# Block transposes of a triangular inverse moved from TensorE to VectorE, and residual parts and a first down product of a mixture of experts moved in the order

## The chip, the core and the metric

The kernel runs on one core of one Trainium2 chip. The metric is the device time of one execution in microseconds (us). The core has a matrix engine (TensorE, PE in the rows), a vector engine (VectorE, DVE), a scalar engine (ScalarE, ACT), GpSimd (POOL) and an engine that issues most transfers (SyncE, SP). Each takes its own instructions in the order in which they were laid down, and waits at an instruction whose inputs or buffers are not ready.

## What is computed

Two transformer blocks over 256 tokens of width 1024, batch 1, all in 32 bit floats. The change touches two parts of the first block. One is a recurrence over time for 8 heads of width 64:

```python
def step(state, inp):
    r_t, k_t, v_t, kk_t, b_t, d_t = inp
    sa = jnp.einsum('bhvk,bhk->bhv', state, -kk_t)
    state = (state * d_t[:, :, None, :] + sa[..., None] * b_t[:, :, None, :]
             + v_t[..., None] * k_t[:, :, None, :])
    return state, jnp.einsum('bhvk,bhk->bhv', state, r_t)
```

The other is a mixture of 32 experts in 4 groups, of which each token takes 2 of one group:

```python
for e in range(N_EXPERTS):
    hidden = jax.nn.silu(t @ w_gate[e]) * (t @ w_up[e])
    y = y + combine[:, e:e + 1] * (hidden @ w_down[e])
```

## The kernel before

**The recurrence** (`rwkv2`) is computed in two chunks of 128 steps. In a chunk the steps of a head are coupled by a lower triangular 128x128 matrix, and the kernel needs the inverse of one minus it: 8 heads by 2 chunks make 16 such matrices. They lie four to a tile of 128x512, so there are four tiles, called lanes (`lane[0]` to `lane[3]`). The running inverse of a lane is `G`. It starts as the inverse of 8x8 blocks on the diagonal, and three levels (`for lv in (8, 16, 32)`, L1033) double the blocks. In a level, for each lane, TensorE multiplies `L` and `G` (`prod`, L1002: four 128x128 products of 32 bit, eight instructions), and VectorE masks the result into `Z` (`both`, L1015). TensorE also transposes `G` into a bank of its accumulator memory (L1039, four instructions), and ScalarE copies that out as `T` (`copy`, L1008). Then in a second pass over the lanes TensorE multiplies `T` and `Z`, and VectorE adds the product to `G`. During these levels `G` is zero outside 32x32 blocks on the diagonal. The last doubling, to 128, works on 64x64 pieces (L1049 to L1067), with copies of 64x256 by VectorE and ScalarE.

Behind it comes the **chain** over the two chunks. It begins with `heads(AkT, ...)`, products of the values `V` with a matrix that does not depend on `G`: eight for chunk 0 into the banks `px`, copied out as `X[0]`, and eight for chunk 1. Then `solve(0, f)` multiplies the inverse with `X[0]`, and so on (L1138 to L1199). There are eight accumulator banks in all.

**The experts** (class `Moe`). Every weight block is loaded in 32 bit, 1 MB at a time, and each 128x512 piece of it is split in two: ScalarE rounds it to a high part `whi` (L304), and VectorE subtracts that to get the low part `wlo` (L308). TensorE then makes three products of each piece (`mm3`, L297 to L299). An expert has 8 pieces for gate and up (`gate_up`) and 4 for the down product (`down`). Between the two, `hidden` applies silu on ScalarE (L1512) and the weight of the expert on VectorE (L1513), and `turn` transposes the result on TensorE (L1520) and splits it into `hh` and `hl`. The code lays the work down by a pipeline: in step t come `turn(t-1)`, `gate_up(t)`, `down(t-1)`. Expert 0 is irregular, for its hidden values need the router's weights: `combine`, `weights(0)`, `hidden(0)` and `turn(0)` are called inside `gate_up(1)`. A scheduler of the language then sets each engine's order from this code, so what stands in an order is read from the built program.

The tokens of a group are collected by products with a 0/1 matrix `D` (`gather`). Groups 0 and 1 are gathered in front. Groups 2 and 3 are gathered in four portions, one at the end of each `down(e)` for e = 9 to 12. A portion needs 256 columns of the tokens `x`, themselves split into a high and a low part by `cut`. The low part of portions 0 and 2 is made by VectorE, and that of portions 1 and 3 by GpSimd (`on_pool`, L306), since `cut` gets `b % 2`.

The stream of blocks (`moe_blocks`) has the order in which the pieces are used; split pieces live in nine pairs of buffers (`K.hl`, `K.hl2`), which the parts of `cut` share.

Of the kernel before, what the change touches and what calls it, by code (L numbers as in the profile page):

```python
# [256 lines left out]
def bank(K):  # L257
    return K.ps.tile([128, 512], F32, name="ps", tag="ps")
# [679 lines left out]
def rwkv2(K, mixh, mixl, tmp_pool, done):  # L938


    nc = K.nc
# [3 lines left out]
    with tmp_pool("rw_i", 1) as pool:  # L945
# [59 lines left out]
        def copy(src, act):  # L1005
            t = sq_()
            if act:
                nc.scalar.activation(t, src, AF.Copy)  # L1008
            else:
                nc.vector.tensor_copy(t, src)  # L1010
            return t
# [21 lines left out]
        for lv in (8, 16, 32):  # L1033
            for q in range(4):
                d = lane[q]
                d["Z"] = both(prod(L[q], d["G"]), bc(c[f"Z{lv}"], 1, 4), OP.mult)
                p = bank(K)
                for u in range(4):
                    nc.tensor.transpose(p[:, u * 128:u * 128 + 128], d["G"][:, u, :], K.ident)  # L1039
                d["T"] = copy(p.rearrange("p (u s) -> p u s", u=4), True)  # L1040
                yield 1.3
            for q in range(4):
                d = lane[q]
                d["G"] = both(prod(d.pop("T"), d.pop("Z")), d["G"], OP.add)
                yield 0.9

        for q in range(4):
            d = lane[q]
            p = bank(K)  # L1049
            pt = bank(K)  # L1050
            for u in range(4):
                nc.tensor.matmul(p[LOP, u * 64:u * 64 + 64], L[q][HIP, u, 0:64], d["G"][HIP, u, 64:128], start=True, stop=True)
            for u in range(4):
                nc.tensor.transpose(pt[LOP, u * 64:u * 64 + 64], d["G"][LOP, u, 0:64], K.ident[LOP, 0:64])
            zt = sq_()
            d["Z"], d["T"] = zt[LOP, :, 0:64], zt[LOP, :, 64:128]
            nc.vector.tensor_copy(d["Z"], p[LOP, :256].rearrange("p (u s) -> p u s", u=4))
            nc.scalar.activation(d["T"], pt[LOP, :256].rearrange("p (u s) -> p u s", u=4), AF.Copy)
            yield 0.7
        for q in range(4):  # L1060
            d = lane[q]
            p = bank(K)
# [10 lines left out]


        G = [d["G"] for d in lane]
        un = lambda h, j: (h // 4 * 2 + h % 2, h // 2 % 2 * 2 + j)
        X, U = ([sq_().rearrange("p u s -> p (u s)") for _ in range(2)] for _ in range(2))
        Y = [K.hl.tile([128, 512], F32, name=f"Y{j}", tag="whi") for j in range(2)]
        S = sq_()
# [2 lines left out]
        def own(ap, f=None):  # L1082

            dims = [list(d) for d in ap.ap]
            return bass.AP(tensor=ap.tensor, offset=ap.offset, ap=[dims[0], [256, 2], [192, 2], [1, 64]])

        def heads(W, j, ps, f, r, start, stop):
            for i in range(4):
                h = 4 * f + i
                q, u = un(h, j)  # L1090
                nc.tensor.matmul(ps[:, i * 128:i * 128 + 128], W[q][:, u, :], r[:, h // 2 * 128:h // 2 * 128 + 128],
                                 start=start and i == 0, stop=stop, skip_group_check=True)

        def from_s(ps, s, f, stop):
            for i in range(2):
# [39 lines left out]
            split(K, mixh[:, 4:8, js], mixl[:, 4:8, js], yt)  # L1135
            yield

        px = [bank(K), bank(K)]  # L1138
        for f in range(2):
            heads(AkT, 0, px[f], f, V[:, 0], True, True)  # L1140
            out(px[f], X[0], f, f)
        K.st.fill(4)
        yield 1.7
        px = [bank(K), bank(K)]
        for f in range(2):
            heads(AkT, 1, px[f], f, V[:, 1], True, False)
        yield 1.7
        for f in range(2):
            solve(0, f)
        yield 1.7  # L1150
# [69 lines left out]
def moe_blocks(K):  # L1220

    ins = K.ins
    b = []
    for e in range(33):
        if e < 32:
            b += [([ins[n][0, e].rearrange("(p k) f -> p k f", k=8)[:, k:k + 4] for n in ("w_gate", "w_up")], None, None)
                  for k in (0, 4)]
        if e:  # L1230
            b.append((ins["w_down"][0, e - 1].rearrange("(f p) d -> p f d", p=128), None, None))
    return b


class Moe:
# [203 lines left out]
    def gather(self, g, b):  # L1439


        K = self.K
        nc = K.nc
        gs = slice(g * CAP, (g + 2) * CAP)
        put = (0, 2) if g == 0 else (0, 1)
        at = slice(0, put[1] + 1, put[1])
        if (0, b) not in self.xs:
            self.cut((0, 1), slice(b * 256, b * 256 + 256), b % 2)
        xs = [(j, part) for j in range(2) for part in self.xs.pop((j, b))]
        p = bank(K)  # L1450
        for i in range(2):
            for n, (j, part) in enumerate(xs):
                nc.tensor.matmul(p[:, i * 256:i * 256 + 256], part[:, i * 128:i * 128 + 128], self.D[:, j, gs],
                                 start=n == 0 and i == 0, stop=n == 3, skip_group_check=True)
        out = [(2 * b + i, K.gq[:, 2 * b + i:2 * b + i + 1], p[:, i * 256:i * 256 + 256].rearrange("p (g s) -> p g s", g=2))
               for i in range(2)]
        for k, gain, src in out:
            nc.scalar.activation(self.xh[:, at, k, :], src, AF.Copy, scale=gain)
        for k, gain, src in out:
            nc.vector.scalar_tensor_tensor(self.xl[:, at, k, :], src, gain, self.xh[:, at, k, :].bitcast(F32), op0=OP.mult,  # L1460
                                           op1=OP.subtract)
        for i in range(2):
            self.G[g + i] = [self.xh[:, put[i]], self.xl[:, put[i]]]
# [19 lines left out]
    def gate_up(self, e):  # L1483
        K, st = self.K, self.st
        nc = K.nc
        xh, xl = self.G[e // 8][:2]
        p = bank(K)
        for n in range(8):
            st.fill()
            hi, lo = st.next()[2:]  # L1490
            mm3(nc, p, xh[:, n, :], xl[:, n, :], hi[:, 0, :], lo[:, 0, :], n == 0, n == 7)
            if e == 1 and n == 0:
                drain(self.combine())
            if e == 1 and n == 4:
                self.weights(0)
                self.hidden(0)
            if e == 1 and n == 7:
                self.turn(0)
            if e == 3 and n == 0:
                for j in range(2):  # L1500
                    K.nc.vector.tensor_scalar(self.D[:, j, 2 * CAP:], K.cst["slots"][:, 2 * CAP:], self.sl[:, j:j + 1], None,
                                              op0=OP.is_equal)
            if e % 8 == 0 and n == 5 and e:
                self.weights(e // 8)
        self.st_[e] = p
        if e:
            self.hidden(e)
# [8 lines left out]
    def turn(self, e):  # L1516
# [5 lines left out]
        hl = self.pool.tile([128, 2, 128], F32R, name="hl__", bufs=2)  # L1522
        split(K, hh, hl, p[:, :256].rearrange("p (f s) -> p f s", f=2))
        self.st_[e] = (hh, hl)

    def down(self, e):
        K, st = self.K, self.st
# [1313 lines left out]
def layer1(K, tmp_pool):  # L2841
# [6 lines left out]
    with ExitStack() as es:  # L2848
# [37 lines left out]
            with tc.manual_schedule():  # L2886
                m.front(mix, K.tail)
        K.pool_share = ()
        pipeline(list(range(32)), [lambda e: e and m.turn(e), lambda e: e and m.gate_up(e), m.down, m.count], [1, 0, 1, 1])
        K.rings = [ring2]  # L2890
        m.rest()
        spare = [t.rearrange("p k t -> p (k t)") for t in spare_raw(K)]
# [41 lines left out]
```

## Time and profile before

| | us |
|---|---|
| runs shown, median of 3 | 1280.58 (1280.01 to 1281.12) |
| profiled execution, its own time | 1280.19 |
| its span in the trace | 1278.3 |

Times inside the trace count from the start of the span; the profiled execution has 1.9 us outside it. A row of the timeline gives start, length, engine, line, operation, tiles written and read, shape and count; rows of one kind that follow each other are merged. [...]

### The profile page before, as it was taken

What the parts mean: (1) busy time and instruction counts of PE and PEld (TensorE: products, weight loads), DVE (VectorE), ACT (ScalarE), POOL (GpSimd) and SP (SyncE); (2) the same over time, 40 slices, a digit from 0 to 9 for tenths busy, and PEclk for the clock granted to TensorE, in tenths of its full rate; (3) what the DMA queues carried; (4) which work ended last, traced back from release to release, by engine and by line L of the source; (5) the groups of instructions that cost most, each with busy time, mean ns of one, the idle gap of its engine ahead of it and who ended that gap; (6) DMA issues with size and microseconds to landing.
All of it is one profiled execution on the core that took longest, in us unless ns stands there. A gap on an engine that the chain in (4) does not pass through costs nothing.

```text
span 1278.3 us, 21070 instructions
## 1 busy us (share of the span) xinstructions
PE 1216.7 (95%) x7798; PEld 1063.3 (83%) x7798; DVE 891.3 (70%) x1790; ACT 743.0 (58%) x1532; POOL 161.3 (13%) x245
## 2 busy tenths in 40 slices
PE   7898999989989999989979999999899999999997
PEld 7687998878877888878866899988788878999986
DVE  4688546789979999976966555564465687555452
ACT  6864323679878898864444444554346644555451
POOL 7134002000010000001020000000048322000000
PEclk9899999889989999999999999999999999999999
DMA  9322007688979998646321266565252313665460
GB/s 281 119 100 83 1 2 223 250 290 319 364 262 330 332 388 325 209 141 204 132 67 53 97 198 198 198 217 182 82 153 84 132 34 110 204 192 169 170 228 34
DMA packets 124282, 228.71 MB, mean 179 GB/s; under 512 B 10720, under 2 KB 86832, under 8 KB 124176
## 3 DMA queue, kind: packets, MB, share of 16 engines
q1 hardware_dynamic: 122672, 223.83, 51.5%
q0 software_dynamic: 1504, 3.49, 0.9%
q8 instruction: 63, 1.03, 0.3%
q14 instruction: 43, 0.35, 0.1%
HBM read 226.25 MB, written 1.05 MB: 178 GB/s over the span
## 4 chain that ended last, share of the span: by engine, by line
PE 46%; DVE 5%; ACT 2%; issue 1%; POOL 1%; DMA 1%; DVEq 0%; POOLq 0%; ACTq 0%
PE ps L299 13%; PE ps L297 13%; PE ps L298 13%; PE ps L2686 1%; DVE wlo L308 1%; PE ps L2615 1%; PE ps L2651 1%; ACT whi L304 1%; PE ps L2505 1%; DMA raw<-in_ev_w_in_dram 1%; PE ps L1918 1%; PE ps L2137 1%; DVE acc L2084 0%; PE ps L2193 0%; PE ps L2616 0%
## 5 line engine op out<-in xcount | busy, mean ns | idle before, releaser
L308 DVE TENSOR_TENSOR wlo<-raw,whi 128x512 fp32r<-128x512 f32 (+1 forms) x797 | 510.3, 689 | 77.4 <-ACT whi L304 75.2
L304 ACT ACTIVATE whi<-raw 128x512 fp32r<-128x512 f32 (+1 forms) x821 | 476.5, 625 | 113.5 <-PE ps L299 37.8
L297 PE MATMUL ps<-hTh,whi 128*128 128x256 f32 (+1 forms) x1032 | 301.2, 292 | 1.2 <-ACT whi L304 1.2
L299 PE MATMUL ps<-hTh,wlo 128*128 128x256 f32 (+1 forms) x1032 | 292.3, 283 | 0.2 <-DVE wlo L308 0.2
L298 PE MATMUL ps<-hTl,whi 128*128 128x256 f32 (+1 forms) x1032 | 291.9, 283 | 0.0
L297 PEld LDWEIGHTS ps<-hTh,whi 128*128 128x128 f32 (+1 forms) x1032 | 196.5, 190 | 5.5 <-issue 2.7
L298 PEld LDWEIGHTS ps<-hTl,whi 128*128 128x128 f32 (+1 forms) x1032 | 197.3, 191 | 3.0 <-issue 2.6
L299 PEld LDWEIGHTS ps<-hTh,wlo 128*128 128x128 f32 (+1 forms) x1032 | 196.0, 190 | 0.4 <-DVE wlo L308 0.4
L297 PE MATMUL ps<-whi,xh 128*128 128x512 f32 x256 | 104.2, 407 | 0.0
L298 PE MATMUL ps<-wlo,xh 128*128 128x512 f32 x256 | 101.8, 398 | 0.0
L299 PE MATMUL ps<-whi,xl 128*128 128x512 f32 x256 | 101.7, 397 | 0.0
L272 POOL TENSOR_TENSOR nrs<-nv,mhalf 128x1 f32<-128x1 f32 x10 | 5.6, 557 | 625.1 <-DVE nv L1716 625.1
L304 ACT ACTIVATE hh<-sl 128x512 fp32r<-128x512 f32 x20 | 12.6, 632 | 115.3 <-DVE sl L1808 115.3
L1808 DVE TENSOR_TENSOR sl<-sl,ps 128x512 f32<-128x512 f32 x20 | 13.8, 688 | 88.8 <-PE ps L299 88.8
L298 PE MATMUL ps<-wlo,hh 128*128 128x512 f32 x176 | 69.6, 395 | 0.0
L297 PE MATMUL ps<-whi,hh 128*128 128x512 f32 x176 | 69.3, 394 | 0.0
L297 PE MATMUL ps<-whi,hTh 128*128 128x256 f32 (+3 forms) x192 | 61.1, 319 | 6.3 <-ACT hTh L304 4.4
L299 PE MATMUL ps<-whi,hTl 128*128 128x256 f32 (+3 forms) x192 | 60.2, 314 | 1.3 <-DVE hTl L308 1.3
L298 PE MATMUL ps<-wlo,hTh 128*128 128x256 f32 (+3 forms) x192 | 60.0, 313 | 0.8 <-DVE wlo L308 0.8
L299 PEld LDWEIGHTS ps<-whi,xl 128*128 128x128 f32 x256 | 48.5, 189 | 11.1
L297 PEld LDWEIGHTS ps<-whi,xh 128*128 128x128 f32 x256 | 48.8, 191 | 10.1
L298 PEld LDWEIGHTS ps<-wlo,xh 128*128 128x128 f32 x256 | 48.7, 190 | 9.9
(880 smaller groups left out, 2170.7 us busy)
## 6 DMA issues: line engine op xcount, KB each, us to landing
raw<-in_w_gate_dram SPq DMA_DIRECT2D x64, 512.0 KB, 5.5
raw<-in_w_up_dram SPq DMA_DIRECT2D x64, 512.0 KB, 6.3
raw<-in_w_down_dram SPq DMA_DIRECT2D x32, 1024.0 KB, 7.1
raw<-in_ffn_w_gate_dram SPq DMA_DIRECT2D x22, 1024.0 KB, 5.4
raw<-in_ffn_w_up_dram SPq DMA_DIRECT2D x22, 1024.0 KB, 5.9
raw<-in_ffn_w_down_dram SPq DMA_DIRECT2D x22, 1024.0 KB, 4.9
raw<-in_ev_w_in_dram SPq DMA_DIRECT2D x11, 1024.0 KB, 5.6
raw<-in_od_w_in_dram SPq DMA_DIRECT2D x10, 1024.0 KB, 5.4
```

Of the source, the lines that this page charges most:

```text
L297: nc.tensor.matmul(ps, lh, rh, start=start, stop=False, **kw)
L298: nc.tensor.matmul(ps, lh, rl, start=False, stop=False, **kw)
L299: nc.tensor.matmul(ps, ll, rh, start=False, stop=stop, **kw)
L304: K.nc.scalar.activation(hi, src, AF.Copy)
L308: K.nc.vector.tensor_tensor(lo, src, hi.bitcast(F32), op=OP.subtract)
L1808: nc.vector.tensor_tensor(sl, sl, pu, op=OP.mult)
L1918: nc.tensor.matmul(p2, c[f"R{d}"], z.rearrange("p b t -> p (b t)"), start=True, stop=True)
L2137: nc.tensor.matmul(o(h0, i), qlT[h % 2][:, h // 2, js], ckvT[:, :nk], start=i == 0, stop=False, skip_group_check=True)
L2505: nc.tensor.matmul(p[:, :60], w1[:, i, :], tmp[:, i].rearrange("p g n -> p (g n)"), start=i == 0, stop=i == 15)
L2615: nc.tensor.matmul(o, q2[r], KL[r, b, :, :u.nk], start=False, stop=False, skip_group_check=True)
L2651: nc.tensor.transpose(pt[:, b * 128:b * 128 + 128], u.pr[:, b * 128:b * 128 + 128], K.ident)
L2686: nc.tensor.matmul(o, u.pT[:, bb * 128:bb * 128 + 128], vsw[:, b, s, g * 64:g * 64 + 64], start=b == 0, stop=b == j)
```

## The change

Four things are changed. In the three levels the transposes of `G` on TensorE and their copies on ScalarE give way to one instruction per lane on VectorE, which transposes each 32x32 block of the tile where it stands. The products `heads(AkT, ...)` that began the chain are issued in the first loop of the last doubling, eight instructions behind each lane; their four banks are taken there. In the experts, the residual parts of portions 0 to 3 are cut in `gate_up` of experts 10 to 13 behind piece 4, all by VectorE, and the gathers use them. `weights(0)` and `hidden(0)` come two pieces later in `gate_up(1)`, `turn(0)` moves into `gate_up(2)`, and `down(0)` runs right before `down(1)`, with its block of weights moved back in the stream accordingly.

```diff
@@ rwkv2, the three levels
                 d["Z"] = both(prod(L[q], d["G"]), bc(c[f"Z{lv}"], 1, 4), OP.mult)
-                p = bank(K)
-                for u in range(4):
-                    nc.tensor.transpose(p[:, u * 128:u * 128 + 128], d["G"][:, u, :], K.ident)
-                d["T"] = copy(p.rearrange("p (u s) -> p u s", u=4), True)
-                yield 1.3
+                d["T"] = sq_()
+                nc.vector.transpose(*(t.rearrange("p u s -> p (u s)") for t in (d["T"], d["G"])))
+                yield 0.9
@@ last doubling, first loop (un and heads moved up, unchanged)
+        px = [[bank(K), bank(K)] for _ in range(2)]
...
-            yield 0.7
+            heads(AkT, q // 2, px[q // 2][q % 2], q % 2, V[:, q // 2], True, q < 2)
+            yield 1.6
@@ the chain
-        px = [bank(K), bank(K)]
         for f in range(2):
-            heads(AkT, 0, px[f], f, V[:, 0], True, True)
-            out(px[f], X[0], f, f)
+            out(px[0][f], X[0], f, f)
         K.st.fill(4)
         yield 1.7
-        px = [bank(K), bank(K)]
-        for f in range(2):
-            heads(AkT, 1, px[f], f, V[:, 1], True, False)
-        yield 1.7
+        px = px[1]
@@ moe_blocks
-        if e:
-            b.append((ins["w_down"][0, e - 1].rearrange("(f p) d -> p f d", p=128), None, None))
+        for d in () if e < 2 else (0, 1) if e == 2 else (e - 1,):
+            b.append((ins["w_down"][0, d].rearrange("(f p) d -> p f d", p=128), None, None))
@@ Moe.gather
-            self.cut((0, 1), slice(b * 256, b * 256 + 256), b % 2)
+            self.cut((0, 1), slice(b * 256, b * 256 + 256), False)
@@ Moe.gate_up
-            if e == 1 and n == 4:
+            if e == 1 and n == 6:
                 self.weights(0)
                 self.hidden(0)
-            if e == 1 and n == 7:
+            if e == 2 and n == 1:
                 self.turn(0)
...
+            if 10 <= e < 14 and n == 4:
+                b = e - 10
+                self.cut((0, 1), slice(b * 256, b * 256 + 256), False)
@@ new, called in the pipeline in the place of down
+    def downs(self, e):
+        for d in () if e == 0 else (0, 1) if e == 1 else (e,):
+            self.down(d)
```

**VectorE, first loop of the first level** (`ps` are banks, `cst_l` holds the masks, `bd` are the 128x512 tiles). Before, four masked products and then a sum:

```order
L1015 TENSOR_TENSOR bd_1838<-ps_1833,cst_l_368 128x512
L1015 TENSOR_TENSOR bd_1852<-ps_1847,cst_l_368 128x512
L1015 TENSOR_TENSOR bd_1866<-ps_1861,cst_l_368 128x512
L1015 TENSOR_TENSOR bd_1880<-ps_1875,cst_l_368 128x512
L1015 TENSOR_TENSOR bd_1894<-ps_1889,bd_1810 128x512
```

Now:

```order
L1015 TENSOR_TENSOR bd_1838<-ps_1833,cst_l_368 128x512
L1039 STREAM_TRANSPOSE bd_1840<-bd_1810 128x512
L1015 TENSOR_TENSOR bd_1847<-ps_1842,cst_l_368 128x512
L1039 STREAM_TRANSPOSE bd_1849<-bd_1817 128x512
L1015 TENSOR_TENSOR bd_1856<-ps_1851,cst_l_368 128x512
L1039 STREAM_TRANSPOSE bd_1858<-bd_1824 128x512
L1015 TENSOR_TENSOR bd_1865<-ps_1860,cst_l_368 128x512
L1039 STREAM_TRANSPOSE bd_1867<-bd_1831 128x512
L1015 TENSOR_TENSOR bd_1874<-ps_1869,bd_1810 128x512
```

A level has 8 instructions of this width on VectorE before and 12 now, each transpose behind the mask of its lane. On TensorE the rows of L1039 are gone and nothing else moved between the products of the levels.

**TensorE, from the end of expert 1's gate and up** (`comb` are the router's weights, `hd` hidden values, `xh` and `xl` the gathered tokens). Before:

```order
L299 MATMUL ps_2823<-whi_2884,xl_2385 128x512
L1473 MATMUL ps_2908<-comb_2382,D_2383 128x33 x2
L1475 MATMUL ps_2908<-cst_i_90,D_2383 128x128 x2
L1520 MATMUL ps_2945<-cst_i_90,hd_2918 128x128 x2
L297 MATMUL ps_2955<-whi_2894,hh__2948 128x512
```

Now:

```order
L299 MATMUL ps_2763<-whi_2824,xl_2326 128x512
L1470 MATMUL ps_2865<-comb_2323,D_2324 128x33 x2
L1472 MATMUL ps_2865<-cst_i_90,D_2324 128x128 x2
L1520 MATMUL ps_2888<-cst_i_90,hd_2885 128x128 x2
L297 MATMUL ps_2895<-whi_2834,xh_2325 128x512
L298 MATMUL ps_2895<-wlo_2835,xh_2325 128x512
L299 MATMUL ps_2895<-whi_2834,xl_2326 128x512
L297 MATMUL ps_2895<-whi_2841,xh_2325 128x512
L298 MATMUL ps_2895<-wlo_2842,xh_2325 128x512
L299 MATMUL ps_2895<-whi_2841,xl_2326 128x512
L1520 MATMUL ps_2910<-cst_i_90,hd_2875 128x128 x2
```

The weights still stand behind the last product of expert 1. The first transposes behind them are now those of expert 1's hidden values, which VectorE makes second; expert 2's products follow them, where before the down product of expert 0 waited for the split of what was transposed.

**VectorE, around expert 10's hidden value** (`raw` is a loaded block, `x` the tokens, `hd` the hidden value, `hl` the low part of the transposed one). Before:

```order
L308 TENSOR_TENSOR wlo_3942<-raw_3654,whi_3941 128x512
L1513 SCALAR_TENSOR_TENSOR hd_3938<-hd_3938,cw_3686,ps_3875 128x256
L308 TENSOR_TENSOR wlo_3949<-raw_3654,whi_3948 128x512
L308 TENSOR_TENSOR wlo_3956<-raw_3654,whi_3955 128x512
L308 TENSOR_TENSOR wlo_3965<-raw_3695,whi_3964 128x512
L308 TENSOR_TENSOR wlo_3972<-x_1497,whi_3971 128x512
L308 TENSOR_TENSOR hl___3992<-ps_3988,hh__3991 128x256
```

Now:

```order
L308 TENSOR_TENSOR wlo_3855<-x_1497,whi_3854 128x512
L308 TENSOR_TENSOR wlo_3859<-raw_3556,whi_3858 128x512
L308 TENSOR_TENSOR wlo_3866<-raw_3556,whi_3865 128x512
L308 TENSOR_TENSOR wlo_3876<-raw_3594,whi_3875 128x512
L1513 SCALAR_TENSOR_TENSOR hd_3882<-hd_3882,cw_3626,ps_3815 128x256
L308 TENSOR_TENSOR wlo_3886<-raw_3594,whi_3885 128x512
```

The first residual part (`wlo_3972` before, `wlo_3855` now) moved from the fourth place behind expert 10's hidden value to the fourth ahead of it. Three more rows like it now stand at the same place ahead of the hidden values of experts 11 to 13, where before there was one more, behind expert 12's. On TensorE the eight instructions of each gather now stand in one run behind a down product.

## Rows read from the trace of the kernel before

**Rows 1.** The page, part 1: busy us, share, instructions by engine.

```profile
PE 1216.7 (95%) x7798; PEld 1063.3 (83%) x7798; DVE 891.3 (70%) x1790; ACT 743.0 (58%) x1532; POOL 161.3 (13%) x245
```

**Rows 2.** Timeline, TensorE, levels to chain: start, length, line, tiles, count.

```profile
150.69 1.06 PE L1002 MATMUL ps<-bd,L 128*128 128x128 f32 x8
...
151.58 0.60 PE L1039 MATMUL ps<-cst_i,bd 128*128 128x128 f32 x4
...
152.02 1.06 PE L1002 MATMUL ps<-bd,L 128*128 128x128 f32 x8
...
176.57 0.68 PE L1052 MATMUL ps<-bd,L 64*64 64x64 f32 x8
...
182.36 3.84 PE L1091 MATMUL ps<-Vn,AkT 128*128 128x128 f32 x32
...
186.03 1.95 PE L1091 MATMUL ps<-bd 128*128 128x128 f32 x16
```

**Rows 3.** By stretch: PE, PEld, DVE, ACT, POOL busy; clock; DMA share; GB/s.

```profile
149.36:176.57 27.21, 27.21 (x247) 27.04 (x245) 17.02 (x26) 7.64 (x13) 0.53 (x1) 1.00 0.01 2
260.67:267.49 6.82, 6.20 (x16) 4.56 (x17) 3.61 (x8) 2.16 (x4) 0.00 (x0) 0.50 0.51 166
359.66:366.48 6.82, 5.78 (x18) 5.01 (x19) 2.04 (x5) 2.89 (x6) 0.98 (x1) 0.50 0.75 285
```

**Rows 4.** Timeline, VectorE, same levels; the bracket is idle before, with releaser.

```profile
150.45 0.69 DVE L1015 TENSOR_TENSOR bd<-ps,cst_l 128x512 f32<-128x512 f32 x1 [0.20 <-PE ps L1002]
...
151.78 0.69 DVE L1015 TENSOR_TENSOR bd<-ps,cst_l 128x512 f32<-128x512 f32 x1 [0.64 <-PE ps L1002]
```

**Rows 5.** Timeline, VectorE, later: dense and strided rows of this width.

```profile
218.36 4.90 DVE L308 TENSOR_TENSOR wlo<-raw,whi 128x512 fp32r<-128x512 f32 x8
...
230.75 1.08 DVE L308 TENSOR_TENSOR yh<-x,yh 128x512 fp32r<-128x512 f32 x1 [2.44 <-ACT yh L304]
```

**Rows 6.** Timeline, TensorE, experts 0 and 1 and the first down product.

```profile
245.90 0.40 PE L297 MATMUL ps<-whi,xh 128*128 128x512 f32 x1
...
256.79 0.39 PE L299 MATMUL ps<-whi,xl 128*128 128x512 f32 x1
257.87 0.60 PE L1473 MATMUL ps<-comb,D 128*128 128x33 f32 x4 [0.69 <-DVE comb L1421]
...
260.82 0.66 PE L1520 MATMUL ps<-cst_i,hd 128*128 128x128 f32 x2 [2.09 <-DVE hd L1513]
261.95 0.79 PE L297 MATMUL ps<-whi,hh__2948 128*128 128x512 f32 x1 [0.47 <-ACT hh__2948 L304]
```

**Rows 7.** Timeline, VectorE, hidden values of experts 0 and 1.

```profile
260.20 0.87 DVE L1513 SCALAR_TENSOR_TENSOR hd<-hd,cw,ps 128x256 f32<-128x256 f32 x2
```

**Rows 8.** Timeline, TensorE, gathers of the third group (two windows).

```profile
360.70 0.58 PE L1453 MATMUL ps<-D,wlo 128*128 128x256 f32 x1 [3.38 <-POOL wlo L306]
...
384.39 0.39 PE L1453 MATMUL ps<-D,wlo 128*128 128x256 f32 x1 [1.35 <-POOL wlo L306]
```

**Rows 9.** Timeline, GpSimd, same stretch.

```profile
356.70 3.94 POOL L306 TENSOR_TENSOR wlo<-x,whi 128x512 fp32r<-128x512 f32 x1 [120.96 <-ACT whi L304]
```

**Rows 10.** Timeline, ScalarE, hidden values of experts 2, 3, 10, 11, 12, 14.

```profile
273.34 0.47 ACT L1512 ACTIVATE hd<-ps,cw 128x256 f32<-128x256 f32 x1
...
281.92 0.47 ACT L1512 ACTIVATE hd<-ps,cw 128x256 f32<-128x256 f32 x1
...
344.67 0.47 ACT L1512 ACTIVATE hd<-ps,cw 128x256 f32<-128x256 f32 x1
...
354.44 0.47 ACT L1512 ACTIVATE hd<-ps,cw 128x256 f32<-128x256 f32 x1
...
370.24 0.47 ACT L1512 ACTIVATE hd<-ps,cw 128x256 f32<-128x256 f32 x1
...
391.33 0.47 ACT L1512 ACTIVATE hd<-ps,cw 128x256 f32<-128x256 f32 x1
```

**Rows 11.** Timeline, VectorE, a residual part of expert 10's stretch.

```profile
347.38 1.21 DVE L308 TENSOR_TENSOR wlo<-x,whi 128x512 fp32r<-128x512 f32 x1
```

More of the change, by code (lines that the diff above doesn't have):

```diff
@@ L1045, in rwkv2, with heads @@
                 yield 0.9
+        un = lambda h, j: (h // 4 * 2 + h % 2, h // 2 % 2 * 2 + j)
+        def heads(W, j, ps, f, r, start, stop):
+            for i in range(4):
+                h = 4 * f + i
+                q, u = un(h, j)
+                nc.tensor.matmul(ps[:, i * 128:i * 128 + 128], W[q][:, u, :], r[:, h // 2 * 128:h // 2 * 128 + 128],
+                                 start=start and i == 0, stop=stop, skip_group_check=True)
+        px = [[bank(K), bank(K)] for _ in range(2)]
         for q in range(4):
@@ L1075, in rwkv2 @@
         G = [d["G"] for d in lane]
-        un = lambda h, j: (h // 4 * 2 + h % 2, h // 2 % 2 * 2 + j)
         X, U = ([sq_().rearrange("p u s -> p (u s)") for _ in range(2)] for _ in range(2))
@@ L1085, in own @@
             return bass.AP(tensor=ap.tensor, offset=ap.offset, ap=[dims[0], [256, 2], [192, 2], [1, 64]])
[L1087 to L1092, printed above, removed]
         def from_s(ps, s, f, stop):
@@ L2888, in layer1 @@
         K.pool_share = ()
-        pipeline(list(range(32)), [lambda e: e and m.turn(e), lambda e: e and m.gate_up(e), m.down, m.count], [1, 0, 1, 1])
+        pipeline(list(range(32)), [lambda e: e and m.turn(e), lambda e: e and m.gate_up(e), m.downs, m.count], [1, 0, 1, 1])
         K.rings = [ring2]
```

## Prediction

> **What bounds the kernel now.** I read the page first: TensorE is busy 95% of the span, VectorE 70%, ScalarE 58%, GpSimd 13% [rows 1]. So a change gains where it takes work or idle time from TensorE, and the question in each stage is whether the engine that takes the work over has room. I then read the timeline of TensorE in the stages the change touches. In the inverse's levels TensorE has no gap at all: 27.21 us busy in a stretch of 27.21, with VectorE at 17.02 and ScalarE at 7.64 [rows 3]. One product of four matrices takes 0.89 us until the next instruction (150.69 to 151.58) and the four transposes 0.44 (151.58 to 152.02) [rows 2]. VectorE waits for TensorE there, 0.64 us ahead of a mask [rows 4]. In the experts the rhythm is TensorE's too: from the first to the last of the 48 products of experts 0 and 1 it takes 10.89 us, 0.232 each [rows 6], and an undisturbed expert takes 8.58 us, from 273.34 to 281.92 [rows 10]. Three places break that rhythm: behind expert 1, TensorE waits 0.69, 2.09 and 0.47 us [rows 6]; at two of the later gathers it waits 3.38 and 1.35 us for a low part that GpSimd makes [rows 8], one of which lasts 3.94 us [rows 9]. [...]
>
> **Part 1, the transposes.** Removed from TensorE: three levels of four transposes, 12 x 0.44 = 5.3 us. Of the stretch of 27.2 us remain 21.9. Removed from ScalarE: 12 copies, which nothing waits for once the transposes are gone. Added to VectorE: 12 instructions of 128x512. No row shows this instruction. The nearest is a dense row of the same width, eight of which take 4.90 us with 0.69 for one, so (4.90 - 0.69) / 7 = 0.60 from one to the next [rows 5]. Strided rows of this width take 1.08 and 1.21 [rows 5, 11], and 1.21 is my other end; nothing excludes it, since a block transpose also changes the order of elements. I take 0.60, because tile and result are dense and of the same type. VectorE then has 36 rows in the three levels instead of 24: 36 x 0.60 = 21.6 us from its first mask at 150.45 [rows 4], to 172.1. TensorE needs only the first lane's last sum to go on, which lies three rows (1.8 us) earlier and is done 0.69 after its start: about 171.0. TensorE's own work ends at 149.36 + 21.9 = 171.3. The two are so close that the fourth lane's transpose comes late by some 0.2 us in two of the levels, since it is the eighth of VectorE's rows between two sums and TensorE by then has finished six products. I put the start of the last doubling at 171.7, where it is 176.57 now [rows 2]. **Gain 4.9**, at most 5.3. At 1.21 a transpose costs (1.21 - 0.69) x 12 = 6.2 more, as VectorE is then the bound: 4.9 - 6.2 = -1.3.
>
> [...]
>
> **Part 2, the chain's beginning.** The 32 instructions that stand from 182.36 to 186.03 [rows 2] are issued earlier, between the lanes of the last doubling. TensorE is full there before and after, so I cost the move at nothing. What it does is cover the copies of the last doubling. Its dangers: four banks are held longer, which leaves four to the lanes, so that two lanes might wait for a copy, at most a dense row's 0.69 each; and `solve` now follows the last products directly, with only its first half, which needs lanes 0 and 1, to cover the copy of lane 3, again at most 0.69. Ends: 0 to 2.1 us lost; I take 0, as the copies are half as wide as these rows.
>
> **Part 3, the residual parts.** From expert 10's hidden value to expert 14's are 46.66 us for four experts with a gather each [rows 10]. The first of the four, 344.67 to 354.44, took 9.77, and it is the case after the change: one gather and one residual part on VectorE, 1.21 us long [rows 11]. Four such make 39.1. **Gain 7.6.** It holds the two waits (4.7) and what the half clock cost behind the first. The best end is TensorE alone: 8.58 and eight products of 256 columns at half of 0.232 give 9.51, so 46.66 - 38.0 = 8.6. The worst end: VectorE has no room for the two parts GpSimd gives up, 2 x 1.21 = 2.4 come through in full, gain 5.2. What hides them is that a part is wanted by no one until the end of the next down product, and that VectorE stands pieces ahead of TensorE. If that lead is used up, expert 13's gate and up products are late first.
>
> **Part 4, expert 0's down product.** TensorE still waits for the weights and then for a hidden value. It is now the second of two that take 0.87 us together from 260.20 [rows 7], about 0.4 later than the first. In return TensorE goes on with products whose pieces are ready, and the 0.47 us wait for the split [rows 6] is gone. **Gain 0.1.** The stretch at half clock behind it holds the same amount of work. The blocks of weights change their order but not their number, and 0.51 of the transfer engines' time is used in that stretch [rows 3], so I cost the reordering at nothing.
>
> **Sum.** 4.9 + 7.6 + 0.1 = 12.6. The profiled execution took 1280.19 us (span 1278.3 and 1.9 around it), 0.4 below the median of the runs shown. 1280.2 - 12.6 = **1267.6 us**. What lies behind follows TensorE and shifts with it. Everything behind 150 us starts at other times, so a stretch at half clock can come out half as long again or half as short; 6.82 us of it cost 3.4 us of work, so 1.7 us either way. With the ends of the parts the forecast's own range is 1264.0 to 1271.5.
>
> **Rivals.**
> - *A block transpose is dear.* The instruction costs as the strided rows do, VectorE becomes the bound of the levels, and TensorE waits for each lane's `T`. Part 1 gives -1.3 instead of 4.9: 1273.8 us. [...] For it: no row shows this instruction. Against it: dense operands. Chance 0.20.
> - *VectorE becomes the bound of experts 10 to 13.* The two parts come through in full and TensorE, waiting in small pieces, again falls to the lower clock once: part 3 gives 7.6 - 2.4 - 3.4 = 1.8, the time is 1273.4. For it: VectorE works nearly without a pause there. Against it: the 9.77 us of the first of the four. Chance 0.12.
> - *Part 1 does not do what it says*: the levels are held by the sequence product, mask, product, sum of a lane, not by TensorE's work, and the time of the transposes returns as waits. Part 1 gives 0: 1272.5. Against it: four lanes and no idle time now. Chance 0.05.
> - *Slower.* One mechanism at one place: VectorE in the three levels. The transposes eat all other gains once one takes more than 0.69 + 12.6 / 12 = 1.74 us, two and a half times the dense row's 0.69. At four times, 2.76, the levels lose 12 x 2.07 = 24.8 against the sum: 1292.4. Against it: no row of 128x512 on VectorE read here is over 1.21. Chance 0.04.
>
> **Numbers.** The forecast has 0.59. The range 1263.5 to 1275.5 holds it, the second and third rival and most of the first, to a transpose of 1.35 us, for 1275.5 - 1267.6 = 7.9 = 12 x 0.66; outside are the slower case, the dearest transposes and the tails, together some 0.15. A measurement of this kernel tells 0.2%, 2.6 us, from no change. Faster by more than that holds for all cases but the fourth and a small rest of the first: 0.93. Within: 0.03. Slower: 0.04.
>
> **What would show it.** Twelve transposes of about 0.69 us on VectorE; the last doubling some 22 us behind the first level's first product; TensorE with small gaps of tenths, on the fourth lane, in the levels; no residual part on GpSimd; ScalarE's hidden values of experts 10 to 14 about 39 us apart, and the granted clock at 1.00 between them; behind expert 1 one wait of some 2.4 us, with a slow stretch as before. The prediction is wrong if transposes are over 1 us long, if the four experts take over 42 us, or if the gained time comes back as a longer wait in a later stage.

## The result and the profile after

The changed kernel takes 1264.97 us (median of 4 runs, 1263.55 to 1266.80), the kernel before beside it 1280.30. The ratio is 0.9885, with a 95% interval from 0.9866 to 0.9904: faster by 12 to 17 us, where 12.6 were forecast. The profiled execution took 1266.2 us, with a span of 1264.4. That is 13.9 below the span before.

Part 1 of the page; it answers to [rows 1]:

```profile
PE 1210.1 (96%) x7750; PEld 1058.5 (84%) x7750; DVE 894.8 (71%) x1804; ACT 734.8 (58%) x1520; POOL 156.1 (12%) x243
```

TensorE has 48 instructions fewer (12 groups of four transposes), VectorE 14 more, ScalarE 12 fewer. The stretches that answer to [rows 3], in the same columns (length, then PE, PEld, DVE, ACT and POOL busy, the clock TensorE was granted as a share of the full one, so that 0.50 is half clock, DMA share, GB/s): the levels, the stretch behind expert 1, and the four experts with a gather.

```profile
148.72:170.60 21.88, 21.88 (x197) 21.72 (x195) 21.48 (x38) 0.47 (x1) 0.52 (x1) 1.00 0.01 2
256.71:260.12 3.41, 3.18 (x9) 2.53 (x10) 1.92 (x5) 1.01 (x2) 0.00 (x0) 0.50 0.86 289
338.75:376.85 38.10, 38.10 (x185) 31.73 (x184) 38.04 (x68) 36.52 (x68) 0.00 (x0) 1.00 0.94 317
```

In the levels TensorE is still busy all the time, and VectorE now is too: 21.48 of 21.88. In the four experts TensorE has no idle time and the full clock. Their ends are ScalarE's hidden values, as in [rows 10]:

```profile
338.75 0.47 ACT L1512 ACTIVATE hd<-ps,cw 128x256 f32<-128x256 f32 x1
...
376.85 0.47 ACT L1512 ACTIVATE hd<-ps,cw 128x256 f32<-128x256 f32 x1
```

VectorE's timeline in the levels, for [rows 4]; L1039 is the new transpose:

```profile
150.43 0.70 DVE L1039 STREAM_TRANSPOSE bd<-bd 128x512 f32<-128x512 f32 x1
151.05 0.65 DVE L1015 TENSOR_TENSOR bd<-ps,cst_l 128x512 f32<-128x512 f32 x1
151.62 0.69 DVE L1039 STREAM_TRANSPOSE bd<-bd 128x512 f32<-128x512 f32 x1
152.24 0.65 DVE L1015 TENSOR_TENSOR bd<-ps,cst_l 128x512 f32<-128x512 f32 x1
```

A transpose takes 0.69 to 0.70 us and the next row starts 0.62 later, nearly as behind a dense row (0.60 [rows 5]). TensorE's timeline from the last doubling to the chain, for the second half of [rows 2]:

```profile
170.60 0.68 PE L1061 MATMUL ps<-bd,L 64*64 64x64 f32 x8
171.20 0.41 PE L1063 MATMUL ps<-cst_i,bd 64*64 64x64 f32 x4
171.54 1.16 PE L1051 MATMUL ps<-Vn,AkT 128*128 128x128 f32 x8
172.63 0.67 PE L1061 MATMUL ps<-bd,L 64*64 64x64 f32 x8
...
175.61 1.16 PE L1051 MATMUL ps<-Vn,AkT 128*128 128x128 f32 x8
176.61 0.38 PE L758 MATMUL ps<-cst_i,omla 128*128 128x128 f32 x2
...
180.96 2.05 PE L1051 MATMUL ps<-bd 128*128 128x128 f32 x16
182.85 1.95 PE L1051 MATMUL ps<-Vn,RkT 128*128 128x128 f32 x16
...
184.63 0.39 PE L1155 MATMUL ps<-Vn,kn__320 128*128 128x128 f32 x2
```

And behind expert 1, for [rows 6]:

```profile
252.52 0.39 PE L299 MATMUL ps<-whi,xl 128*128 128x512 f32 x1
253.60 0.60 PE L1470 MATMUL ps<-comb,D 128*128 128x33 f32 x4 [0.69 <-DVE comb L1418]
...
256.94 0.66 PE L1520 MATMUL ps<-cst_i,hd 128*128 128x128 f32 x2 [2.48 <-DVE hd L1513]
```

From the starts of such rows comes a ledger of the two profiled executions. Here "state" is the first product of the chain's state (L1155 at 184.63 after, shown above; L1158 before, shown below), "weights" is 257.87 and 253.60, and the last product of the program starts at 1270.50 and 1256.59.

```profile
189.61 0.39 PE L1158 MATMUL ps<-Vn,kn__320 128*128 128x128 f32 x2
```

| stretch on TensorE | before | after | gained |
|---|---|---|---|
| start to the levels' first product | 149.36 | 148.72 | 0.64 |
| levels, to the last doubling | 27.21 | 21.88 | 5.33 |
| last doubling to state | 13.04 | 14.03 | -0.99 |
| state to weights | 68.26 | 68.97 | -0.71 |
| weights to hidden value 10 | 86.80 | 85.15 | 1.65 |
| hidden value 10 to 14 | 46.66 | 38.10 | 8.56 |
| from there to the last product | 879.17 | 879.74 | -0.57 |

Parts 1 and 2 gave 4.3 (4.9 forecast), part 3 gave 8.6 (7.6), part 4 at most 1.65 (0.1). The first, fourth and last lines hold no changed work. The granted clock is 0.50 there for other lengths: up to the levels for 10.24 us before and 6.83 after, between state and weights for 10.24 and 13.65, and behind the four experts for 13.65 and 17.07. In each of the three lines the kernel with less of it is ahead.

### The profile page after: what moved, and what is told of

Same layout as the page of the kernel before. It is cut to its first block, busy times and chain, and to the rows that moved or that the text cites. A ratio compares the mean times of both kernels' runs of the same rounds, so it can differ in the third digit from the quotient of the medians.

```text
span 1264.4 us, 20959 instructions
## 1 busy us (share of the span) xinstructions
PE 1210.1 (96%) x7750; PEld 1058.5 (84%) x7750; DVE 894.8 (71%) x1804; ACT 734.8 (58%) x1520; POOL 156.1 (12%) x243
## 4 chain that ended last, share of the span: by engine, by line
PE 47%; DVE 5%; ACT 2%; issue 1%; POOL 1%; DMA 0%; DVEq 0%; POOLq 0%; ACTq 0%
PE ps L299 13%; PE ps L297 13%; PE ps L298 13%; PE ps L2690 1%; DVE wlo L308 1%; PE ps L2619 1%; PE ps L2655 1%; ACT whi L304 1%; PE ps L2509 1%; PE ps L1922 1%; PE ps L2141 1%; DMA raw<-in_ev_w_in_dram 0%; DVE acc L2088 0%; PE ps L2197 0%; PE ps L2620 0%
## 5 line engine op out<-in xcount | busy, mean ns | idle before, releaser
L304 ACT ACTIVATE hh<-sl 128x512 fp32r<-128x512 f32 x20 | 12.6, 632 | 115.3 <-DVE sl L1812 115.3
```

Source lines behind the costliest of these rows:

```text
L304: K.nc.scalar.activation(hi, src, AF.Copy)
```

## Experiments

The kernel before was run beside each, and each ratio is to it: 1281.09 us (14 runs) for parts 1, 3 and 4 alone and for the changed kernel with the chain late, 1278.99 (19) for who and when, each transpose twice, and both waits away, 1278.51 (16) for part 2 alone and for the last two versions of both waits away. The recorded expectations count the experiments in this order: the fourth is the changed kernel with the chain late, the eighth the version with both waits away, the tenth that version with the chain late.

### Part 1 alone

The kernel before with this and nothing else:

```diff
-                p = bank(K)
-                for u in range(4):
-                    nc.tensor.transpose(p[:, u * 128:u * 128 + 128], d["G"][:, u, :], K.ident)
-                d["T"] = copy(p.rearrange("p (u s) -> p u s", u=4), True)
-                yield 1.3
+                d["T"] = sq_()
+                nc.vector.transpose(*(t.rearrange("p u s -> p (u s)") for t in (d["T"], d["G"])))
+                yield 0.9
```

> The kernel before with the transposes of the three levels on VectorE and nothing else. Theory: part 1 is worth what TensorE no longer does, and it is kept to the end: the levels' first product to the last doubling takes 21.9 us instead of 27.2, the solve starts 5.3 to 6 us earlier than at 186.03, and the whole is 1275.0, 5.3 below the kernel before, give or take the 1.7 us of half a stretch at half clock. Rival: the gain is lost again before the experts, because the stages behind the inverse wait for VectorE or for weights: the gathers then start less than 4 us earlier and the whole is 1277 or more.

Measured: 1273.86 us, ratio 0.9952 (0.9929 to 0.9975), so 6.1 of 1281.09 with 3.2 to 9.1 as its interval. By stretches, the levels and what came behind them:

```profile
148.41:170.28 21.87, 21.87 (x196) 21.71 (x194) 21.47 (x38) 0.48 (x1) 0.52 (x1) 1.00 0.01 2
175.55:182.37 6.82, 6.82 (x37) 6.31 (x35) 1.86 (x5) 0.86 (x2) 0.00 (x0) 0.50 0.01 2
```

The levels give what they give in the changed kernel. The second row had not been expected: the clock fell to 0.50 in the last doubling, among products of 64x64. From the last doubling to the state it takes 16.66 us, where the same instructions take 13.55 at full clock (the changed kernel with the chain late, below), so this took back 3.1, and the state starts only 2.67 earlier than before. The gathers start 2.72 earlier and the interval reaches the rival's 1277, so both of its signs are there; but from state to gathers it takes 51.28 us (51.33 before), so nothing is lost to waits of the rival's kind. Its mechanism falls. The whole has the theory's size, but in the profiled execution, 5.9 lower, 2.5 of that come behind the four experts, where it is at 0.50 for 6.83 us instead of 13.65.

### Part 3 alone

The kernel before with `False` in place of `b % 2` at the gather, and in `gate_up`:

```diff
+            if 10 <= e < 14 and n == 4:
+                b = e - 10
+                self.cut((0, 1), slice(b * 256, b * 256 + 256), False)
```

> The kernel before with the residual parts of experts 10 to 13 cut by VectorE an expert ahead, and nothing else. Theory: from expert 10's hidden value to expert 14's 38.1 us instead of 46.66, as in the changed kernel, with no granted clock of 0.50 in between; the whole 1271.7, 8.6 lower. Rival: in the changed kernel the four experts profit from the lead that the other parts give VectorE; alone the parts come through, 40.5 us for the four experts and 1274 for the whole.

Measured: 1272.75 us, ratio 0.9934 (0.9915 to 0.9954), 8.5 lower. The four experts by stretch:

```profile
346.68:384.78 38.10, 38.10 (x185) 31.73 (x184) 38.05 (x68) 36.53 (x69) 0.00 (x0) 1.00 0.95 319
```

38.10 us, the changed kernel's own figure, without the other parts' help. The rival falls.

### Who cuts, and when

Part 3 does two things. The first of these kernels has only the `False` at the gather; the second has only the cut in `gate_up`, with `b % 2` for its last argument, so that GpSimd still makes the second and the fourth part.

> The kernel before with all four residual parts cut by VectorE, but at the gather itself, not an expert ahead. Theory: what costs is GpSimd's duration, so who cuts is most of it; each of the four experts then takes what those with an even gather take now, 9.77 to 9.93 us, 39.4 from expert 10's hidden value to expert 14's instead of 46.66, no half clock, and the whole is 1273.8, 7.3 below the kernel before. Rival: the time of the cut is most of it; the part on VectorE stands behind pieces of weights that it has to make first, TensorE waits 1 us or more at each gather, and the four experts take 42 us or more.

> The kernel before with the residual parts cut an expert ahead, but the second and fourth of them still by GpSimd. Theory: a part of 3.94 us that is begun half an expert (over 4 us) ahead is hidden whoever makes it, so there is no wait at the gathers and the four experts take 38.1 to 38.5 us, the whole 1272.5. Rival: GpSimd's instruction holds VectorE up while it runs, so that 1 us or more per odd gather returns as late pieces: 40 us or more.

Measured: 1274.63 us, ratio 0.9967 (0.9957 to 0.9977), and 1271.82, ratio 0.9950 (0.9933 to 0.9967). The four experts by stretch, for the cut by VectorE at the gather:

```profile
345.78:384.79 39.01, 38.93 (x185) 31.43 (x184) 38.70 (x67) 36.62 (x68) 0.00 (x0) 1.00 0.92 320
```

and for the cut ahead, half of it by GpSimd:

```profile
344.22:382.32 38.10, 38.10 (x185) 31.73 (x184) 38.04 (x65) 36.49 (x68) 3.65 (x2) 1.00 0.91 319
```

GpSimd's own timeline there:

```profile
351.22 1.94 POOL L306 TENSOR_TENSOR wlo<-x,whi 128x512 fp32r<-128x512 f32 x1 [114.53 <-ACT whi L304]
370.26 1.71 POOL L306 TENSOR_TENSOR wlo<-x,whi 128x512 fp32r<-128x512 f32 x1 [17.10 <-ACT whi L304]
```

Either half is nearly enough: 46.66 falls to 39.01 by who alone, to 38.10 by when alone. Cutting ahead is what gives the last 0.9, and then GpSimd does as well. The forecast saw the gain in taking the work from GpSimd, which is not wrong but not needed. One thing was not tried: GpSimd's parts took 1.94 and 1.71 us here, so whether one of 3.94 would be hidden too is not shown.

For the whole the first of the two missed its expectation: 4.2 us lower (2.9 to 5.5) instead of 7.3, though its stretch is 7.65 shorter. The stretch at 0.50 at the second gather is gone, and yet the mean granted clock of its runs is not higher than that of the kernel before (0.9805 over 10 runs, 0.9814 over 19), so it was at 0.50 for longer elsewhere. Its trace shows one such place, in the last doubling and the chain's first products, which nothing here changes and where the trace of the kernel before has full clock:

```profile
179.65:186.47 6.82, 6.82 (x49) 6.68 (x48) 2.29 (x6) 0.38 (x1) 0.00 (x0) 0.50 0.00 0
```

### Part 4 alone

The kernel before with the new order of blocks, `downs`, and the calls moved (the change's own lines).

> The kernel before with expert 0's down product behind expert 1's, and nothing else. Theory: the step itself is worth 0.1 to 0.5 us (the 0.47 us wait for the split goes, the second hidden value comes 0.4 later), so the whole is 1279.8 to 1280.2, no difference that can be measured; that the stretch at half clock behind it was 3.41 us long in the changed kernel instead of 6.83 was chance. Rival: the shorter stretch is what the step does, since TensorE goes on with products that have their pieces; then it is 3.41 us here too, and the whole is 1278.0 to 1278.6.

Measured: 1280.12 us (10 runs), ratio 0.9995 (0.9981 to 1.0009), no difference that can be measured. From weights (257.77) to hidden value 10 (344.07) it took 86.3 us against 86.80, so 0.5. The stretch behind the wait:

```profile
259.98:266.81 6.83, 5.70 (x16) 4.56 (x17) 4.07 (x10) 2.63 (x6) 0.00 (x0) 0.50 0.55 196
```

It is as long as before [rows 3]. So the theory holds for this run. Over all traces the rival is not dead: of the four with part 4 and this wait (the changed kernel, this one, the one with the chain late and the one with each transpose twice) three show 3.41 us of 0.50 behind this wait, and the six without part 4 all show 6.82 or 6.83.

### Part 2, from three sides

First the changed kernel with the chain's 32 first products back behind the last doubling:

```diff
-            heads(AkT, q // 2, px[q // 2][q % 2], q % 2, V[:, q // 2], True, q < 2)
-            yield 1.6
+            yield 0.7
...
+            heads(AkT, 0, px[f], f, V[:, 0], True, True)
```

> The changed kernel with the chain's 32 first products back behind the last doubling, where the kernel before has them. Theory: in the changed kernel the interleaved products cost about 1.0 us (TensorE is 5.97 us ahead of the kernel before at the last doubling and 4.97 at the solve); here the solve is again 5.9 ahead, at about 180.1, and the whole is 1264.0. Rival, that the interleaving is needed: without it TensorE waits for the copies of the last doubling, now that the lanes stand closer, the solve starts at 181 or later and the whole is 1265.5 or more.

Measured: 1266.86 us, ratio 0.9894 (0.9878 to 0.9911), beside 0.9885 for the changed kernel. TensorE's timeline:

```profile
171.44 0.67 PE L1051 MATMUL ps<-bd,L 64*64 64x64 f32 x8
...
177.74 3.84 PE L1090 MATMUL ps<-Vn,AkT 128*128 128x128 f32 x32
181.41 1.95 PE L1090 MATMUL ps<-bd 128*128 128x128 f32 x16
```

No gap: the 32 products take 3.67 us up to the solve, where the four groups of eight in the changed kernel take 1.09, 1.09, 1.00 and 1.08, in all 4.26. From the last doubling to state it is 13.55 instead of 14.03. So nothing needed the interleaving as a cover, and it costs TensorE 0.5, less than the theory's 1.0. The solve at 181.41 and the whole above 1265.5 are the rival's figures and not the theory's (180.1 and 1264.0), but without the rival's wait: in this trace the levels already begin 0.85 later (149.57 against 148.72). By ratio the two kernels cannot be told apart. By then the granted clock was the suspect: the products of 64x64 stand alone here, and in five of seven traces like this the clock had fallen to 0.50 between the last doubling and the solve, for 3.41 us or some 6.8. So part 2 was run alone, on the kernel before:

> The kernel before with the chain's 32 first products issued between the lanes of the last doubling, and nothing else. So far the traces with these products behind the last doubling show the granted clock at 0.50 for 3.41 or 6.83 us between the last doubling and the solve in five of seven cases (not in the kernel before's own nor in the fourth experiment's), and the three with the products between the lanes in none. Theory: the early beginning costs TensorE 4 x (1.09 - 0.92) = 0.7 us and keeps the clock up, which is worth 2.2 on average: no 0.50 from the last doubling to the solve here, and the whole 1.5 below the kernel before, 0.1%. Rival: the stretches there are chance, the early beginning only costs its 0.7, and the whole is the kernel before's or 0.7 above it.

Measured: 1278.83 us (12 runs), ratio 0.9999 (0.9988 to 1.0010). Its timeline:

```profile
175.71 0.68 PE L1062 MATMUL ps<-bd,L 64*64 64x64 f32 x8
176.32 0.41 PE L1064 MATMUL ps<-cst_i,bd 64*64 64x64 f32 x4
176.66 1.16 PE L1052 MATMUL ps<-Vn,AkT 128*128 128x128 f32 x8
177.75 0.67 PE L1062 MATMUL ps<-bd,L 64*64 64x64 f32 x8
...
189.53 0.39 PE L1156 MATMUL ps<-Vn,kn__320 128*128 128x128 f32 x2
```

13.82 us from the last doubling to state, against 13.04: the price of the move is 0.8. There is no 0.50 from the last doubling to the solve in this trace, but the mean granted clock is 0.982 over its 12 runs and 0.982 over the 16 of the kernel before, so a gain of 2.2 us by the clock does not show in it. The rival is nearer.

### Both waits behind expert 1 away

The changed kernel still waits 0.69 and 2.48 us there. This version lets TensorE go on with expert 2's pieces:

```diff
-            if e == 1 and n == 6:
+            if e == 2 and n == 2:
                 self.weights(0)
                 self.hidden(0)
-            if e == 2 and n == 1:
+                self.hidden(1)
+            if e == 2 and n == 5:
                 self.turn(0)
+                self.turn(1)
...
-        if e:
+        if e > 1:
             self.hidden(e)
```

and the pipeline calls `turn` itself only from expert 2 on.

> The changed kernel with the weights, both first hidden values and their two turns moved into expert 2's products (after its third and its sixth piece), so that TensorE goes on with pieces instead of waiting 1.08 us for the combining weights and 2.75 us for the hidden value of expert 1. Theory: both waits go, and so does the stretch at half clock behind them (3.41 us, worth 1.7); the gain is 3.8 + 1.7 = 5.5 and the whole is 1259.5. Rival: in the waits VectorE gets ahead with pieces (0.81 us each with the routing's small rows between them, where TensorE needs 0.70), so the waits are only handed on to the pieces of expert 2: gain under 2 us, 1263 or more.

Measured: 1257.94 us (1256.62 to 1258.97), ratio 0.9844 (0.9828 to 0.9861). **This version beats both kernels**, the changed one by 5.2 us going by the two ratios, where 5.5 were expected. The same place on TensorE's timeline, and then the stretch in the columns of [rows 3]:

```profile
252.54 0.40 PE L299 MATMUL ps<-whi,xl 128*128 128x512 f32 x1
252.78 0.53 PE L1470 MATMUL ps<-comb,D 128*128 128x33 f32 x4
253.14 0.41 PE L1472 MATMUL ps<-cst_i,D 128*128 128x128 f32 x2
253.31 0.48 PE L297 MATMUL ps<-whi,xh 128*128 128x512 f32 x1
```

```profile
249.00:263.00 14.00, 14.00 (x67) 11.39 (x67) 13.54 (x34) 13.59 (x28) 0.00 (x0) 1.00 0.89 300
```

No wait and no half clock in the stretch. VectorE is at 13.54 of 14.00, so it just keeps up; the rival falls. The last two runs are this version with part 2 undone, and this version again beside it:

> The version of the eighth experiment with the chain's first products back behind the last doubling. Theory, that the early beginning keeps the clock up: 1.5 us above that version, 1259.5. Rival, that it only costs TensorE 0.7: 1257.2, and no 0.50 in the trace from the last doubling to the solve.

> The version of the eighth experiment beside the two before it on one chip: 1257.9, 1.5 below the tenth by the theory that the early beginning keeps the clock up, 0.7 above it by the rival. From the gathers to the first product that goes back no gap of 0.7 us or more on TensorE.

Measured: 1260.55 us with the chain late, ratio 0.9858 (0.9838 to 0.9877), and 1258.29 with it early, ratio 0.9828 (0.9810 to 0.9845). That is 2.3 in favour of the early beginning, the theory's sign, though the intervals overlap. The mean granted clock of the runs differs too, 0.984 with the chain late and 0.987 with it early, but not at the last doubling in the trace of the late one, which has full clock from there to state:

```profile
171.13:184.68 13.55, 13.55 (x147) 12.61 (x147) 5.65 (x13) 2.75 (x7) 0.00 (x0) 1.00 0.00 1
```

The early one takes 14.03 there. From the gathers to the first product that goes back its TensorE has no gap of 0.7 us or more, as expected. Over all thirteen traces the clock was at 0.50 between the last doubling and the solve in five of the eight with these products late and in none of the five with them early. Part 2 alone showed no difference in time. **Whether part 2 is worth anything stays open**; that it costs TensorE 0.5 to 0.8 us is shown.

### Each transpose twice

The changed kernel with `for _ in range(2):` ahead of the transpose.

> The changed kernel with each of the 12 block transposes done twice, the second over the first. Theory: VectorE's 36 rows of the levels last as long as TensorE's work (21.6 against 21.9 us), so that each added one comes through with its spacing of 0.60: 48 rows x 0.60 = 28.8 us for the levels instead of 21.9, TensorE waits in every lane, and the whole is 6.9 higher, 1271.9, or 1273.5 to 1275.3 if the waits bring half clock. Rival: VectorE has room (it waits for TensorE ahead of masks), and half of it or more is hidden: levels of 25 us or less, whole under 1268.5.

Measured: 1272.03 us, ratio 0.9953 (0.9936 to 0.9970), 8.7 above the changed kernel going by the two ratios. The levels by stretch, and then TensorE's group of second products there (count, busy us, mean ns, idle us before, with the releaser):

```profile
148.26:178.50 30.24, 24.57 (x196) 22.47 (x194) 29.43 (x49) 0.47 (x1) 0.52 (x1) 1.00 0.00 1
```

```profile
L1002 PE MATMUL ps<-bd 128*128 128x128 f32 x98 | 13.9, 284 | 5.7 <-DVE bd L1040 5.7
```

8.4 us more in the levels, 0.70 for each added transpose, and TensorE waits 5.7 us for them. The expected 28.8 left out the 1.1 us until VectorE's first mask (149.35) and a row of other work on VectorE in between (L761, 0.46). The rival falls: VectorE had no room left in the levels.

## Why the prediction was right

- **Transposes: right.** The choice of the dense row's 0.60 held (0.62 behind a transpose, 0.57 to 0.58 behind a mask). The row itself is 0.69 us, as long as a dense one, and not the 1.08 and 1.21 of the strided ones [rows 5, 11]. The step on the fourth lane's transpose, late by 0.2 us in two of the levels, was wrong: TensorE shows no gap. The levels gave 5.33, of which 0.31 are two transposes of other work (L758) that stood ahead of the last doubling before (176.26) and stand inside it now (176.61): 5.0 where 4.9 were forecast and 5.3 were the best end. That the two engines end almost together was right, as the doubled transposes show.
- **The chain's beginning: the cost of nothing was wrong.** The prediction looked for waits (banks, copies), and none came. What it missed is that the moved instructions take longer by being moved: eight of 128x128 take 1.09 us between products of 64x64, 1.00 where transposes of 128x128 follow them, and 3.67 / 4 = 0.92 in one row. So a change of shape cost some 0.1 us here, an estimate from 1.09 - 1.00. Part 2 alone cost 0.8. In the ledger the last doubling to state lost 0.99; 0.31 of that are the two transposes just named, 0.6 is 4.26 against 3.67 for the four groups, and 0.1 is the solve's first sixteen products, which now stand behind products of 64x64 (180.96 to 182.85, 1.89 us, against 186.03 to 187.82, 1.79, before).
- **Residual parts: the mechanism right, the size 1.0 too small.** The term was 4 experts as long as the first of the four, 9.77 us. That one is not the case after the change: its part was cut at the gather. The run with all four cut there by VectorE has 39.01 us in all, which is the forecast's 39.1. Cut ahead, they take 38.10, 9.5 each and the term's best end, in this trace and in those of both runs above that cut ahead. The rival that VectorE becomes the bound needed its lead to run out, and it did not.
- **The first down product: the size right alone, the half clock behind it not.** The later hidden value came as said, with a wait of 2.48 us instead of 2.09. Alone the step gave 0.5 in its trace and nothing measurable in the whole. "The stretch at half clock behind it holds the same amount of work" held in that run, and failed in the changed kernel, where the stretch was 3.41 us and not 6.82. The forecast had allowed 1.7 us for it either way, and that is about what came.
- **The rest** gave back 0.6 of the sum in stretches without changed work, by lengths of half clock that differ from run to run. Taken singly, the four parts have the ratios 0.9952, 0.9934, 0.9995 and 0.9999, whose product is 0.9880; all together have 0.9885. Within their intervals they add up.

The range held the time, 2.6 us below the likeliest value. Half of that is in the profiled execution, whose gain of 13.9 stands against a sum of 12.6: 0.1 more by part 1, 0.7 less by part 2, 1.0 more by part 3, 1.5 more by part 4 with its shorter stretch, and 0.6 less elsewhere. Most of the 1.5 and all of the 0.6 hang on the clock. That these and the misses of parts 2 and 3 partly cancel is luck. The other half, 1.2, lies between that execution (1266.2) and the median of its four runs. One sum of the prediction does not come out: the ends of its parts, with 1.7 for the clock, add up to 1264.5 to 1273.8 and not to the 1264.0 to 1271.5 it gives as its own range. The time lies in both.

## What to carry to other kernels

When work moves between engines, ask first whether the new engine's row count in that stage fits, then whether the row is dense (0.69 us here, against 1.08 and 1.21 for the strided ones); here 36 dense rows fitted beside TensorE's 21.9 us with nothing to spare, and each of 12 more cost 0.70. A part that is wanted at a fixed place should be made some pieces ahead of it; then it mattered little here which engine made it (38.10 us either way). Room between the making and the use of a value, given also to the waits behind expert 1 that the change left, was worth another 5 us. A moved product is not free because its engine is full before and after: here TensorE took 0.5 to 0.8 us more for the same products once they alternated with others of another shape.

## What the runs showed that was not expected

- The 128x512 transpose of 32 bit elements takes VectorE 0.69 us, as long as a subtraction of that size. Four 128x128 transposes on TensorE took 0.44.
- The clock's stretches at 0.50 do not follow from the program alone. The version without the two waits was profiled twice, and between state and weights it was at 0.50 for 6.83 us the first time and for 10.24 the second:

```profile
229.97:236.80 6.83, 6.46 (x26) 5.74 (x25) 5.69 (x28) 0.94 (x3) 0.61 (x1) 0.50 0.79 268
...
227.40:237.64 10.24, 10.24 (x42) 9.42 (x42) 8.20 (x33) 3.57 (x6) 2.09 (x2) 0.50 0.53 180
```

  The kernel with part 1 alone and the changed kernel with the chain late have the same instructions in the inverse and the chain; the first shows 6.82 us of 0.50 in the last doubling and the chain's first products, the second none. One kernel's runs spread accordingly: the one with GpSimd ahead has runs from 1267.92 us at a mean granted clock of 0.986 to 1278.49 at 0.977.
- One and the same instruction on GpSimd, the strided subtraction of 128x512, took 3.94 us [rows 9] and 2.00 in the kernel before, and 1.94 and 1.71 where it was issued ahead. The long one (356.70 to 360.64) ended 1.4 us behind six rows that VectorE made without a pause (355.58 to 359.27, 0.6 each). Around the one of 1.94 (351.22 to 353.16) it was VectorE that was late: three rows took 3.36 us (350.35 to 353.71), where three in a row take 1.89 in the changed kernel (344.88 to 346.77). What held either engine up was not tried by itself and is not shown.
